# Branch B's mask sums on GpSimd: made one unit ahead, behind the scaling of the unit in front

## The chip, the cores and the metric

The kernel runs on one core of a Trainium2 chip. The metric is the device time of one execution in microseconds (us). The engines are named as the profile names them: PE is TensorE, DVE VectorE, ACT ScalarE, POOL GpSimd, SP SyncE. Each engine works through its own list of instructions in order, and an instruction starts when the semaphores that it waits for have come.

## What is computed

One encoder layer over two sequences, of 1024 and of 512 tokens. Its token mixer has two branches, and the change lies in branch B: attention in a two-dimensional neighbourhood, where each query sees a window of keys on a grid of 64 columns, with a learned bias by relative position. Per block of queries:

```python
s = jnp.einsum('bqhd,bkhd->bhqk', qi, kb, preferred_element_type=jnp.float32) * scale + bias[None]
s = jnp.where(mask[None, None], s, NEG_INF)
p = jax.nn.softmax(s, axis=-1)
return jnp.einsum('bhqk,bkhd->bqhd', p.astype(vb.dtype), vb)
```

Around it stand the norms, the projections, branch A (grouped-query attention over all tokens), sigmoid gates on both branches, the output projection, and an MLP with squared relu. All of it is float32; the kernel keeps that precision by splitting each operand into a high and a low part and adding three products.

## The kernel before

The kernel first runs the token mixer of the short sequence (first trunk, 512 tokens), then that of the long one (second trunk, 1024 tokens), then the MLP over all 1536 tokens. In each trunk branch B is a loop over **units**. A unit is one head with one strip of 16 grid columns and both halves of the rows (second trunk: 8 heads x 4 strips in the order 1, 2, 0, 3, that is 32 units) or one head with two strips (first trunk: strips 1 and 2, then 0 and 3, that is 16 units). Either way a unit has two score products, x = 0 and 1.

`s_unit(u)` makes, for x = 0 and 1 one after the other:

- the mask sum `bm` on GpSimd (line 993): the head's relative bias, gathered for 128 queries in the tile `rect`, plus the mask `msk`, which holds 0 or -1e30. Strip 2 uses the sums of strip 1, so there are 24 sums in the first trunk (128x256) and 48 in the second (128x384). There are four buffers for them;
- the score product on PE (line 1007, two matmuls, high and low part of the keys) into one half of the PSUM tile `s`, which both x share;
- on VectorE `tensor_tensor_reduce` (line 1009): scores plus mask sum, negated, with the row's extreme in `nm_`;
- on ScalarE the exponential with the row's sum (line 1013), on VectorE the reciprocal of the sum (line 1016), on GpSimd the scaling of the row (line 1017).

`t_unit`, one unit later, transposes the scaled rows on PE (lines 1032 and 1038) and splits them into high and low part on ScalarE and VectorE (lines 1041 and 1042). `v_unit`, two units later, multiplies them with the values (line 1064) and adds the parts up (VectorE line 1071, GpSimd line 1084). Between these steps PE is given matmuls of the gate and of the query, key and output projections (`fill`), and VectorE and ScalarE the splits of those weights (lines 198 and 192). `prep(h)` loads `rect` (line 908, two buffers) and the head's value strips (line 914) on SyncE's queue.

The order on the engines is not the order of the code. A scheduler moves instructions on each engine by its own estimate of when they can start, except those that `tc.keep_in_program_order` pins to their place behind what was issued before them on the engine. The mask sums were not pinned: the scheduler put them as far ahead as their four buffers allow, which on GpSimd often means between two scalings of an earlier unit.

Of the kernel before, what the change touches and what calls it, by code (L numbers as in the profile page):

```python
# [11 lines left out]
F32 = mybir.dt.float32  # L12
# [3 lines left out]
ALU = mybir.AluOpType  # L16
AX = mybir.AxisListType

P = 128
# [42 lines left out]
def encoder(ctx: ExitStack, tc: tile.TileContext, xs, outs, w):  # L62
    nc = tc.nc
# [32 lines left out]
    def big(name):  # L96
        return pbig.tile([P, 1024], F32, tag="big", name=name)
# [84 lines left out]
    def rstd(ss, n, width, name, pin=False):  # L182
        m = sml.tile([P, 8], F32, tag="ms", name=f"ms_{name}")
        op = nc.vector.tensor_scalar(m[:, :n], ss, 1.0 / width, EPS, op0=ALU.mult, op1=ALU.add)  # L184
        if pin:
            tc.keep_in_program_order(op)
        r = sml.tile([P, 8], F32, tag="rs", name=f"rs_{name}")
        nc.gpsimd.tensor_tensor(r[:, :n], m[:, :n], mhalf[:, :n], op=ALU.pow)  # L188
        return r
# [240 lines left out]
    def run(tr, nxt, first):  # L430
        N, x, T, NT, NB = tr.N, tr.x, tr.T, tr.NT, tr.NB
        xh, xl = tr.xh, tr.xl
        rows = T // GRID_W
        halves = rows // 8
# [70 lines left out]
        for g in range(2):  # L505
            with phase(f"phR{N}_{g}") as ph:
# [154 lines left out]
                for tt in range(NT):  # L661
                    tb, j = divmod(tt, 4)
                    nm = f"{N}_{g}_{tt}"
# [13 lines left out]
                    op = nc.sync.dma_start(rt, w["rope"][tt * P : (tt + 1) * P])  # L677
# [3 lines left out]
                    js = slice(j * P, (j + 1) * P)  # L681
# [28 lines left out]
                    r = rstd(ss[:, :5], 5, HD, f"A{nm}", fresh and tt < 2 if first else ahead_)  # L710
# [61 lines left out]
            with phase(f"phA{N}_{g}") as ph:  # L772
                units = [(h, qb) for h in range(4) for qb in range(NB)]
# [40 lines left out]
                for ui, u in enumerate(units):  # L814
                    h, qb = u
# [81 lines left out]
        kr_n = 12 if halves == 2 else 8  # L897
        nkc = kr_n // 4
        nkey = kr_n * 32
        nq = rows * 16  # L900
        with phase(f"phB{N}") as ph:
            msk = ph.tile([P, halves * 3, nkey], BF16, tag="msk", name=f"msk{N}", bufs=1)
            nc.gpsimd.dma_start(msk, w["mask2"] if halves == 2 else w["mask1"])
            rects, strips, bms, PT = {}, {}, {}, {}

            def prep(h):
                rc = ph.tile([P, 16, 48], F32, tag="rect", name=f"rect{N}_{h}", bufs=2)
                nc.sync.dma_start(rc, biases[:, :, h].rearrange("r c i j -> (r c) i j"))
                rects[h] = rc
                v = slot([P, 4, rows // 4, P], F32R, f"vs{N}_{h}")  # L910
                for j in range(4):
                    c0 = (0, 8, 24, 32)[j]
                    for a in range(4):
                        nc.sync.dma_start(
                            v[a * 32 : a * 32 + 32, j, :, :].bitcast(F32),
                            vd[:, h, :].rearrange("(k a c) d -> a c k d", a=4, c=GRID_W)[a, c0 : c0 + 32],
                        )
                strips[h] = v

            def load_qk(pr, hold=None):  # L920
                return (
                    load_cols(win, 768 + pr * P, P, f"bq{N}_{pr}", hold=hold),
                    load_cols(win, 1280 + pr * P, P, f"bk{N}_{pr}", hold=hold),
                )
# [49 lines left out]
            JN = 3 - halves  # L974
            W = halves * P

            def s_unit(u):
                h, js = u
                s = big(f"sb{N}_{h}_{js[0]}")
                p = ph.tile([P, 2, nkey], F32, tag="pb", name=f"pb{N}_{h}_{js[0]}", bufs=2)  # L980
                nm_, l, rl = (
                    sml.tile([P, 8], F32, tag=n_, name=f"{n_}b{N}_{h}_{js[0]}") for n_ in ("ms", "ss", "rs")
                )
                for x, (j, hf) in enumerate((j, hf) for j in js for hf in range(halves)):
                    nm = f"{N}_{h}_{j}_{hf}"
                    ct = (0, 1, 1, 2)[j]
                    c0 = (0, 8, 24, 32)[j]
                    jr = (16, 8, 8, 0)[j]
                    r0 = 0 if hf == 0 else 4
                    ir = 4 if hf == 0 else 0  # L990
                    if j != 2:
                        bm = ph.tile([P, nkey], F32, tag="bm", name=f"bm{nm}", bufs=4)
                        nc.gpsimd.tensor_tensor(
                            bm.rearrange("p (r c) -> p r c", c=32),
                            rects[h][:, ir : ir + kr_n, jr : jr + 32],
                            msk[:, hf * 3 + ct, :].rearrange("p (r c) -> p r c", c=32),
                            op=ALU.add,
                        )
                        bms[hf] = bm
                    bm = bms[hf]  # L1000
                    q0 = j * (T // 4) + hf * P
                    so = s[:, x * 512 : x * 512 + nkey]
                    for i in range(2):
                        kv = qk[h // 2][1][h % 2][:, i, :].rearrange("p (r c) -> p r c", c=GRID_W)[
                            :, r0 : r0 + kr_n, c0 : c0 + 32
                        ]
                        nc.tensor.matmul(so, qk[h // 2][0][:, h % 2, q0 : q0 + P], kv, start=(i == 0), stop=(i == 1))
                    sb = ph.tile([P, nkey], F32, tag="sb", name=f"sbs{nm}", bufs=2)
                    nc.vector.tensor_tensor_reduce(
                        out=sb, in0=so, in1=bm, op0=ALU.add, op1=ALU.min, scale=-1.0, scalar=3e38,  # L1010
                        accum_out=nm_[:, x : x + 1],
                    )
                    nc.scalar.activation(
                        p[:, x], sb, AF.Exp, bias=nm_[:, x : x + 1], scale=-1.0, accum_out=l[:, x : x + 1]
                    )
                    nc.vector.reciprocal(rl[:, x : x + 1], l[:, x : x + 1])
                    nc.gpsimd.tensor_scalar(p[:, x], p[:, x], rl[:, x : x + 1], 1.0, op0=ALU.mult, op1=ALU.mult)
                PT[u] = p
# [87 lines left out]
            units = [(h, js) for h in range(8) for js in groups]  # L1106
            n = len(units)
# [4 lines left out]
            for i in range(n + LS + LV):  # L1112
                if NB == 1:
                    f = 9 if i < 1 else 5 if i < n - 4 else 6 if i < n else 4 if i == n else 2
                else:
                    f = 0 if i == n - 10 else 5 + (i % 3 > 0) if i < n - 8 else 7
                if i < n:
                    s_unit(units[i])
                    if units[i][1][0] == 1 and units[i][0] + 1 < 8:
                        prep(units[i][0] + 1)  # L1120
                    if i % per == (6 if JN == 1 else 2) and i + 2 < n:
                        while held:
                            held.pop(0)()
                        qp = qkproj(i // per + 1, wqk, qk)
                        for _ in range(NC8):
                            next(qp)
                    if i % per == per - 1 and qp is not None:
                        for _ in qp:
                            pass
                        qp = None  # L1130
                fill.pull(f // 2)
                if 0 <= i - LS < n:
                    t_unit(units[i - LS])
                if held:
                    held.pop(0)()
                if i % per == 0 and i // per < 3:
                    wqk = load_qk(i // per + 1, held)
                if i == n - (6 if first else 9):
                    pa = proj_a(ph, held)
                    next(pa)  # L1140
                if i == n - (4 if JN == 2 else 8):
                    fill.drain()
                    fill.add(pa)
                if qp is not None and NB == 2:
                    for _ in range(NC8):
                        next(qp)
                fill.pull(f - f // 2)
                if 0 <= i - LS - LV < n:
                    v_unit(units[i - LS - LV])
# [4 lines left out]
        with phase(f"phG{N}") as ph:  # L1154
# [36 lines left out]
            for c in range(NC8):  # L1191
# [4 lines left out]
                for tb in range(NB):  # L1196
# [4 lines left out]
                    nm = f"{N}_{c}_{tb}"  # L1201
# [33 lines left out]
            for half in range(2):  # L1235
                wo = wos[half]
                hc = slice(half * 512, half * 512 + 512)
                for tt in range(NT):
                    tb, j = divmod(tt, 4)
                    nm = f"{N}_{half}_{tt}"  # L1240
# [34 lines left out]
                    for k, i in todo:  # L1275
                        js = slice(i * P, (i + 1) * P)
# [13 lines left out]
                    if ht is not None:  # L1290
                        op = nc.vector.tensor_tensor(ht[:, hc], o, xr, op=ALU.add)
# [12 lines left out]
                    if half == 1:  # L1304
# [5 lines left out]
                        if nxt is None:  # L1310
# [10 lines left out]
                            if 3 <= tt <= 5:  # L1321
                                j = tt - 3
# [557 lines left out]
    for i, tr in enumerate(trunks):  # L1880
        run(tr, trunks[i + 1] if i + 1 < len(trunks) else None, i == 0)
# [66 lines left out]
```

## Time and profile before

| | us |
|---|---|
| runs | 2135.02, 2132.51, 2131.47 (median 2132.51) |
| profiled execution | 2131.02 |
| its span, first to last instruction | 2129.2 |
| POOL busy in the span | 390.7 |
| branch B's loop, first trunk | about 165 to 300 us of the span |
| branch B's loop, second trunk | about 785 to 1050 us of the span |

In the rows of the profile a group reads: line, engine, operation, output tile <- input tiles (buffer numbers left out), shape, count, then busy time and the mean of one in ns, then the idle time of the engine just before and what ended it. In the timeline a row begins with the start in us and the duration in us; what stands in square brackets is the engine's idle time before it and what ended that. Tiles of branch B: `sbs` the scores in PSUM, `sbss` the negated sums, `msbs` their extremes, `bms` the mask sums, `pbs` the exponentials, `rsbs` the reciprocals, `ptbs` the transposes, `bhs` their parts, `obs` and `os_Bs` the outputs. A matmul of 512 columns starts some 0.23 us after the one before it when nothing waits, a 128x128 transpose behind another some 0.11 us.

### The profile page before, as it was taken

How to read it: one execution, taken by the hardware profiler on the slowest of the kernel's cores; microseconds unless marked ns; L12 is line 12 of the kernel's file. 1: busy time of each engine (PE TensorE's matmuls, PEld its weight loads, DVE VectorE, ACT ScalarE, POOL GpSimd, SP SyncE). 2: the span in 40 equal slices, each digit the busy share in tenths (PEclk: the TensorE clock that was granted, in tenths of full speed). 3: DMA queues.
4: the chain of work that ended last, by engine and by line, in shares of the span. 5: the costliest groups of instructions: out<-in, count | busy, mean ns of one | idle time of the engine just before them, and what ended most of it. 6: DMA issues, size and time to landing. Idle time of an engine off the chain costs nothing.

```text
span 2129.2 us, 31802 instructions
## 1 busy us (share of the span) xinstructions
PE 2111.4 (99%) x10967; PEld 1847.8 (87%) x10967; DVE 1471.0 (69%) x2810; ACT 1117.3 (52%) x2351; POOL 390.7 (18%) x508
## 2 busy tenths in 40 slices
PE   9999999999999999999999999999999999999998
PEld 8887788988898888888888999999999988888887
DVE  6674686777667754656782977778777777769563
ACT  5664564566537644655431566566555643434352
POOL 3332420433233323433300200003000000000000
PEclk9999999999999999999999999999999999999999
DMA  6445567521221132433472666578444799688561
GB/s 188 136 125 146 156 192 243 189 72 34 59 85 55 40 110 84 124 105 109 142 247 101 212 197 200 155 247 210 159 146 158 260 353 343 214 279 281 168 197 70
DMA packets 319595, 350.92 MB, mean 165 GB/s; under 512 B 31168, under 2 KB 255048, under 8 KB 319433
## 3 DMA queue, kind: packets, MB, share of 16 engines
q1 hardware_dynamic: 277495, 278.86, 41.7%
q10 hardware_dynamic: 36258, 52.98, 7.1%
q0 software_dynamic: 5680, 17.04, 2.9%
q8 instruction: 87, 1.43, 0.3%
q14 instruction: 75, 0.61, 0.1%
HBM read 264.85 MB, written 87.88 MB: 166 GB/s over the span
## 4 chain that ended last, share of the span: by engine, by line
PE 82%; DVE 2%; DMA 1%; issue 1%; ACT 1%; POOL 1%; SPq 0%; ACTq 0%; POOLq 0%; DVEq 0%
PE dn L205 7%; PE dn L203 7%; PE dn L204 7%; PE pTs L827 3%; PE gpss L203 3%; PE gpss L205 3%; PE gpss L204 3%; PE ud L205 2%; PE uc L205 2%; PE ud L204 2%; PE uc L204 2%; PE uc L203 2%; PE ud L203 2%; PE ua L205 2%; PE ua L204 2%; PE ua L203 2%
## 5 line engine op out<-in xcount | busy, mean ns | idle before, releaser
L205 PE MATMUL dn<-wd,al 128*128 128x512 f32 (+1 forms) x624 | 242.6, 389 | 0.0
L204 PE MATMUL dn<-wd,ah 128*128 128x512 f32 (+1 forms) x624 | 242.6, 389 | 0.0
L203 PE MATMUL dn<-wd,ah 128*128 128x512 f32 (+1 forms) x624 | 242.6, 389 | 0.0
L1361 ACT ACTIVATE ah<-ar 128x512 fp32r<-128x512 f32 x168 | 104.7, 628 | 205.8 <-PE dn L204 181.7
L1362 DVE TENSOR_TENSOR al<-ar,ah 128x512 fp32r<-128x512 f32 x168 | 115.4, 692 | 77.8 <-ACT ah L1361 69.4
L204 PEld LDWEIGHTS dn<-wd,ah 128*128 128x128 f32 x624 | 117.2, 188 | 24.3
L205 PEld LDWEIGHTS dn<-wd,al 128*128 128x128 f32 x624 | 117.2, 188 | 24.1
L203 PEld LDWEIGHTS dn<-wd,ah 128*128 128x128 f32 x624 | 117.2, 188 | 24.0
L793 POOL TENSOR_SCALAR ps<-ps,rls 128x1024 f32<-128x1024 f32 (+1 forms) x96 | 96.8, 1010 | 215.6 <-DVE rls L792 205.0
L833 DVE TENSOR_TENSOR ptls<-pTs,pths 128x512 fp32r<-128x512 f32 x160 | 107.7, 686 | 39.3 <-ACT pths L832 38.8
L832 ACT ACTIVATE pths<-pTs 128x512 fp32r<-128x512 f32 x160 | 94.2, 598 | 74.0 <-PE pTs L827 72.1
L787 DVE TENSOR_REDUCE nms<-ss 128x1 f32<-128x1024 f32 (+1 forms) x96 | 99.6, 1039 | 22.2 <-PE ss L785 21.9
L188 POOL TENSOR_TENSOR rs_f<-ms_f,mhalf 128x1 f32<-128x1 f32 x6 | 4.0, 667 | 590.7 <-DVE ms_f L184 590.7
L203 PE MATMUL gpss<-xs_0h,w_gs 128*128 128x512 f32 x256 | 104.9, 410 | 1.5 <-DVE ptls L833 1.3
L790 ACT ACTIVATE ps<-ss,nms 128x1024 f32<-128x1024 f32 (+1 forms) x96 | 93.2, 972 | 23.1 <-DVE nms L787 20.3
L827 PEld LDWEIGHTS pTs<-ident,ps 128*128 128x128 f32 x640 | 78.2, 140 | 28.0 <-POOL ps L793 4.2
L204 PE MATMUL gpss<-xs_0l,w_gs 128*128 128x512 f32 x256 | 101.1, 395 | 0.0
L205 PE MATMUL gpss<-xs_0h,w_gs 128*128 128x512 f32 x256 | 101.0, 395 | 0.0
L827 PE MATMUL pTs<-ident,ps 128*128 128x128 f32 x640 | 98.9, 274 | 1.2 <-DVE ptls L833 0.3
L1361 ACT ACTIVATE A<-S 128x512 fp32r<-128x512 f32 x128 | 76.1, 624 | 30.5 <-DVE S L1424 26.2
L1362 DVE TENSOR_TENSOR A<-S,A 128x512 fp32r<-128x512 f32 x128 | 84.5, 685 | 3.9 <-ACT A L1361 3.9
L1480 ACT ACTIVATE c<-c 128x384 f32<-128x384 f32 x97 | 50.7, 524 | 68.7 <-DVE c L1479 68.6
(352 smaller groups left out, 6403.6 us busy)
## 6 DMA issues: line engine op xcount, KB each, us to landing
ar<-ud SPq DMA_DIRECT2D x120, 512.0 KB
br<-in_w_mlp_down_dram SPq DMA_DIRECT2D x72, 512.0 KB
rawu<-in_w_mlp_up_dram SPq DMA_DIRECT2D x64, 512.0 KB
ud<-c ACTq DMA_DIRECT2D x128, 192.0 KB
raw_gs<-in_w_in_dram SPq DMA_DIRECT2D x32, 512.0 KB
zgs<-sgs ACTq DMA_DIRECT2D x48, 256.0 KB
ud<-cs SPq DMA_DIRECT2D x64, 192.0 KB
raw_os<-in_w_out_dram SPq DMA_DIRECT2D x16, 512.0 KB
```

The costliest lines, as they stand in the source:

```text
L203: nc.tensor.matmul(out, ah, bh, start=start, stop=False, **kw)
L204: nc.tensor.matmul(out, ah, bl, start=False, stop=False, **kw)
L205: nc.tensor.matmul(out, al, bh, start=False, stop=stop, **kw)
L787: nc.vector.tensor_reduce(nm_, s, axis=AX.X, op=ALU.max, negate=True)
L790: nc.scalar.activation(p, s, AF.Exp, bias=nm_, accum_out=l)
L793: nc.gpsimd.tensor_scalar(p, p, rl, 1.0, op0=ALU.mult, op1=ALU.mult)
L827: nc.tensor.transpose(pt[:, j * P : (j + 1) * P], PP[u, j][:, kc * P : (kc + 1) * P], ident)
L832: nc.scalar.activation(hi, pt, AF.Copy)
L833: nc.vector.tensor_tensor(lo, pt, hi.bitcast(F32), op=ALU.subtract)
L1361: nc.scalar.activation(hi, src, AF.Copy)
L1362: nc.vector.tensor_tensor(lo, src, hi.bitcast(F32), op=ALU.subtract)
L1480: nc.scalar.activation(t, t, AF.Relu)
```

## The change

The sums of a unit are moved out of `s_unit` into a function of their own, `masks(u)`. It is called for unit 0 ahead of the loop's first step and for unit i + 1 right after `s_unit` of unit i, and its sums are pinned, so that on GpSimd they stand behind the scalings of unit i. The dictionary of the sums is keyed by unit. The sums themselves, their shapes and their four buffers are the same.

```diff
+            def masks(u):
+                h, js = u
+                for j, hf in ((j, hf) for j in js for hf in range(halves)):
+                    if j == 2:
+                        bms[u, j, hf] = bms[(h, (1,)) if len(js) == 1 else u, 1, hf]
+                        continue
+                    ct = (0, 1, 1, 2)[j]
+                    jr = (16, 8, 8, 0)[j]
+                    ir = 4 if hf == 0 else 0
+                    bm = ph.tile([P, nkey], F32, tag="bm", name=f"bm{N}_{h}_{j}_{hf}", bufs=4)
+                    tc.keep_in_program_order(
+                        nc.gpsimd.tensor_tensor(
...
+                    bms[u, j, hf] = bm
...
-                    if j != 2:
-                        bm = ph.tile([P, nkey], F32, tag="bm", name=f"bm{nm}", bufs=4)
-                        nc.gpsimd.tensor_tensor(
...
-                        bms[hf] = bm
-                    bm = bms[hf]
+                    bm = bms[u, j, hf]
...
+                if i == 0:
+                    masks(units[0])
                 if i < n:
                     s_unit(units[i])
+                    if i + 1 < n:
+                        masks(units[i + 1])
```

What this does to the order on the engines is shown at three places. In the rows a tile's name ends in head, strip and (for a mask sum) half, and then a running number; line 993 is line 990 after the change, line 1007 is 1017, 1017 is 1027, 1032 is 1042 and 1084 is 1094.

On GpSimd, at the start of the first trunk's branch B, before:

```order
L993 TENSOR_TENSOR bms_0_1_0_2264<-rects_0_2151,msks_2149 128x256
L993 TENSOR_TENSOR bms_0_0_0_2351<-rects_0_2151,msks_2149 128x256
L993 TENSOR_TENSOR bms_0_3_0_2360<-rects_0_2151,msks_2149 128x256
L993 TENSOR_TENSOR bms_1_1_0_2403<-rects_1_2280,msks_2149 128x256
L1017 TENSOR_SCALAR pbs_0_1_2260<-pbs_0_1_2260,rsbs_0_1_2263 128x256
L993 TENSOR_TENSOR bms_1_0_0_2515<-rects_1_2280,msks_2149 128x256
L1017 TENSOR_SCALAR pbs_0_1_2260<-pbs_0_1_2260,rsbs_0_1_2263 128x256
```

and after:

```order
L990 TENSOR_TENSOR bms_0_1_0_2259<-rects_0_2151,msks_2149 128x256
L1027 TENSOR_SCALAR pbs_0_1_2262<-pbs_0_1_2262,rsbs_0_1_2265 128x256 x2
L990 TENSOR_TENSOR bms_0_0_0_2280<-rects_0_2151,msks_2149 128x256
L990 TENSOR_TENSOR bms_0_3_0_2282<-rects_0_2151,msks_2149 128x256
L1027 TENSOR_SCALAR pbs_0_0_2351<-pbs_0_0_2351,rsbs_0_0_2354 128x256 x2
L990 TENSOR_TENSOR bms_1_1_0_2369<-rects_1_2284,msks_2149 128x256
```

Before, the sums of strips 0 and 3 of head 0 and one of head 1 stood ahead of the first scaling; now they stand behind the scalings of the unit in front.

On GpSimd in the second trunk, from the output sum of head 0, strip 1, before:

```order
L1084 TENSOR_TENSOR os_Bs_0_1_9291<-os_Bs_0_1_9291 64x256
L1017 TENSOR_SCALAR pbs_0_3_9296<-pbs_0_3_9296,rsbs_0_3_9299 128x384
L993 TENSOR_TENSOR bms_1_0_1_9530<-rects_1_9116,msks_8915 128x384
L1017 TENSOR_SCALAR pbs_0_3_9296<-pbs_0_3_9296,rsbs_0_3_9299 128x384
L1084 TENSOR_TENSOR os_Bs_0_2_9356<-os_Bs_0_2_9356 64x256
L1017 TENSOR_SCALAR pbs_1_1_9361<-pbs_1_1_9361,rsbs_1_1_9364 128x384 x2
```

and after, from the scalings of the same unit:

```order
L1027 TENSOR_SCALAR pbs_0_3_9300<-pbs_0_3_9300,rsbs_0_3_9303 128x384 x2
L990 TENSOR_TENSOR bms_1_1_0_9318<-rects_1_9116,msks_8915 128x384
L990 TENSOR_TENSOR bms_1_1_1_9320<-rects_1_9116,msks_8915 128x384
L1094 TENSOR_TENSOR os_Bs_0_2_9360<-os_Bs_0_2_9360 64x256
L1027 TENSOR_SCALAR pbs_1_1_9365<-pbs_1_1_9365,rsbs_1_1_9368 128x384 x2
```

Before, a sum for two units later stood between the two scalings of unit 0_3; now the two sums of the next unit, 1_1, stand behind them.

On PE, in the first trunk, from the first score product of unit 0_0 (strips 0 and 3 of head 0) to its second, before:

```order
L1007 MATMUL sbs_0_0_2346<-kBs_0_0_2189,qBs_0_2188 128x256 x2
L203 MATMUL gpss_3328_1_0_2342<-xs_0h_158,w_gs_3328_1_2301 128x512
L204 MATMUL gpss_3328_1_0_2342<-xs_0l_160,w_gs_3328_1_2301 128x512
L205 MATMUL gpss_3328_1_0_2342<-xs_0h_158,w_gs_3328_1_2301 128x512
L203 MATMUL gpss_3328_1_0_2342<-xs_0h_158,w_gs_3328_1_2301 128x512
L204 MATMUL gpss_3328_1_0_2342<-xs_0l_160,w_gs_3328_1_2301 128x512
L1007 MATMUL sbs_0_0_2346<-kBs_0_0_2189,qBs_0_2188 128x256 x2
L205 MATMUL gpss_3328_1_0_2342<-xs_0h_158,w_gs_3328_1_2301 128x512
L1032 MATMUL ptbs_0_1_2376<-ident,pbs_0_1_2260 128x128 x4
```

and after:

```order
L1017 MATMUL sbs_0_0_2350<-kBs_0_0_2189,qBs_0_2188 128x256 x2
L203 MATMUL gpss_3328_1_0_2346<-xs_0h_158,w_gs_3328_1_2305 128x512
L204 MATMUL gpss_3328_1_0_2346<-xs_0l_160,w_gs_3328_1_2305 128x512
L205 MATMUL gpss_3328_1_0_2346<-xs_0h_158,w_gs_3328_1_2305 128x512
L203 MATMUL gpss_3328_1_0_2346<-xs_0h_158,w_gs_3328_1_2305 128x512
L204 MATMUL gpss_3328_1_0_2346<-xs_0l_160,w_gs_3328_1_2305 128x512
L205 MATMUL gpss_3328_1_0_2346<-xs_0h_158,w_gs_3328_1_2305 128x512
L1042 MATMUL ptbs_0_1_2378<-ident,pbs_0_1_2262 128x128 x2
L1017 MATMUL sbs_0_0_2350<-kBs_0_0_2189,qBs_0_2188 128x256 x2
L1042 MATMUL ptbs_0_1_2378<-ident,pbs_0_1_2262 128x128 x2
```

The second score product stands one matmul and two transposes further back. The same happens in the first trunk to units 2_0, 3_1, 4_0, 6_0 and 7_1 (in 4_0 by one matmul and three transposes, in 3_1 by eight matmuls, in 6_0 by nine matmuls and four transposes), and in the second trunk to unit 0_0 alone (by two matmuls). Everywhere else PE's order is the same apart from the numbers in names. VectorE's order moves at those same places only. On SyncE the loads of `rect` stand further back, behind the value strips or weight loads that they stood before.

More of the change, by code (lines that the diff above doesn't have):

```diff
@@ L903, in run @@
             nc.gpsimd.dma_start(msk, w["mask2"] if halves == 2 else w["mask1"])
-            rects, strips, bms, PT = {}, {}, {}, {}
+            rects, strips, PT = {}, {}, {}
             def prep(h):
@@ L975, in run @@
             W = halves * P
+            bms = {}
+            def masks(u):
[10 more added lines that the diff above has]
+                        nc.gpsimd.tensor_tensor(
+                            bm.rearrange("p (r c) -> p r c", c=32),
+                            rects[h][:, ir : ir + kr_n, jr : jr + 32],
+                            msk[:, hf * 3 + ct, :].rearrange("p (r c) -> p r c", c=32),
+                            op=ALU.add,
+                        )
+                    )
+                    bms[u, j, hf] = bm
             def s_unit(u):
@@ L985, in s_unit @@
                     nm = f"{N}_{h}_{j}_{hf}"
-                    ct = (0, 1, 1, 2)[j]
                     c0 = (0, 8, 24, 32)[j]
-                    jr = (16, 8, 8, 0)[j]
                     r0 = 0 if hf == 0 else 4
-                    ir = 4 if hf == 0 else 0
-                    if j != 2:
-                        bm = ph.tile([P, nkey], F32, tag="bm", name=f"bm{nm}", bufs=4)
[L993 to L998, printed above, removed]
-                        bms[hf] = bm
-                    bm = bms[hf]
+                    bm = bms[u, j, hf]
                     q0 = j * (T // 4) + hf * P
```

## The prediction

> **What bounds the kernel now.** I read the page first, then the waits of TensorE and GpSimd, then the timeline at places where one unit of branch B hands over to the next.
>
> ```profile
> span 2129.2 us, 31802 instructions
> PE 2111.4 (99%) x10967; PEld 1847.8 (87%) x10967; DVE 1471.0 (69%) x2810; ACT 1117.3 (52%) x2351; POOL 390.7 (18%) x508
> PE 82%; DVE 2%; DMA 1%; issue 1%; ACT 1%; POOL 1%; SPq 0%; ACTq 0%; POOLq 0%; DVEq 0%
> ```
>
> TensorE (PE) is busy all but 17.8 us of the span (2129.2 - 2111.4), and the chain that ended last is 82% PE. GpSimd (POOL) is busy 18%. So a mask sum can change the time only where PE comes to wait for it. Branch B runs twice: the 512-token trunk and the 1024-token trunk, in these two windows.
>
> ```profile
> 165.00:300.00 135.00, 132.67 (x654) 107.35 (x653) 86.70 (x233) 75.43 (x155) 47.01 (x69) 1.00 0.52 154
> 785.00:1050.00 265.00, 262.35 (x1281) 215.85 (x1281) 167.56 (x435) 145.18 (x308) 101.02 (x138) 1.00 0.37 113
> ```
>
> The first two numbers behind a window are its length and PE's busy time: PE idles 2.33 us in the first and 2.65 us in the second, at a granted clock of 1.00. Nearly all of that would have to vanish to win 0.2%. What PE waits for there:
>
> ```profile
> PE sbs L1007 <- DVE msbs L1009: 1.7, 5, 0.5
> PE ptbs L1038 <- POOL pbs L1017: 0.6, 1, 0.6
> ```
>
> The five waits of 1.7 us are the core of the case. A unit has two score products in one PSUM tile, and the second (QK2) starts only when VectorE has read the first together with its mask sum (DVE1). A late mask therefore becomes a PE wait. GpSimd itself, in the second window:
>
> ```profile
> L993 POOL TENSOR_TENSOR bms<-rects,msks 128x384 f32<-128x384 f32 x44 | 41.9, 953 | 71.7 <-DVE msbs L1009 71.7
> L1017 POOL TENSOR_SCALAR pbs<-pbs,rsbs 128x384 f32<-128x384 f32 x64 | 39.1, 612 | 37.2 <-DVE rsbs L1016 30.7 <-ACT pbs L1013 2.0 <-ACT bhs L1041 1.4
> ```
>
> The masks run so far ahead that GpSimd stands 71.7 us waiting for one of the four mask buffers (released by L1009), and the scalings stand behind those waits. No mask is late for VectorE anywhere.
>
> **The change, part by part.** The same 72 sums and 96 scalings remain; nothing is computed twice. What moves: the sums of unit u+1 stand directly behind the scalings of unit u. Their buffers are then long free, so the 71.7 us of waiting goes; in exchange a loop closes through five engines: QK2 of u, VectorE's second read, exponential, reciprocal, scaling, mask of u+1, DVE1 of u+1, QK2 of u+1. I check each hand-over by one formula: end of the second scaling, plus one mask, against the traced start of DVE1. QK2 follows DVE1 closely, so what is late goes to PE in full.
>
> Second trunk, the tightest hand-over (unit 0_3 to unit 1_1):
>
> ```profile
> 808.67 0.16 DVE L1016 RECIPROCAL rsbs<-ssbs 128x1 f32<-128x1 f32 x1 [0.69 <-ACT pbs L1013]
> 808.93 0.58 POOL L1017 TENSOR_SCALAR pbs<-pbs,rsbs 128x384 f32<-128x384 f32 x1
> 809.91 0.56 DVE L1009 CUSTOM_DVE_ANT_0 sbss<-sbs,bms 128x384 f32<-128x384 f32 x1 [1.08 <-PE sbs L1007]
> 810.40 0.08 DVE L1009 DVE_READ_ACCUMULATOR2_ANT msbs<- 128x1 f32 x1
> 810.54 0.61 PE L1007 MATMUL sbs<-kBs,qBs 128*128 128x384 f32 x2
> ```
>
> The scaling starts 0.10 behind its reciprocal and ends at 809.51; a mask of 0.92 (the row at 793.89 below) ends at 810.43, 0.52 behind DVE1's traced start, and QK2 stood only 0.06 behind DVE1's end (810.48). So PE waits 0.5 us. Order on PE and VectorE is unchanged here. The same formula, at the four others that come out late:
>
> ```profile
> 867.67 0.57 POOL L1017 TENSOR_SCALAR pbs<-pbs,rsbs 128x384 f32<-128x384 f32 x1
> 868.69 0.56 DVE L1009 CUSTOM_DVE_ANT_0 sbss<-sbs,bms 128x384 f32<-128x384 f32 x1 [0.69 <-PE sbs L1007]
> 873.73 0.59 POOL L1017 TENSOR_SCALAR pbs<-pbs,rsbs 128x384 f32<-128x384 f32 x1 [1.32 <-DVE rsbs L1016]
> 875.00 0.56 DVE L1009 CUSTOM_DVE_ANT_0 sbss<-sbs,bms 128x384 f32<-128x384 f32 x1 [0.44 <-issue]
> 880.00 0.59 POOL L1017 TENSOR_SCALAR pbs<-pbs,rsbs 128x384 f32<-128x384 f32 x1 [1.31 <-DVE rsbs L1016]
> 881.30 0.56 DVE L1009 CUSTOM_DVE_ANT_0 sbss<-sbs,bms 128x384 f32<-128x384 f32 x1 [0.48 <-issue]
> 944.85 0.59 POOL L1017 TENSOR_SCALAR pbs<-pbs,rsbs 128x384 f32<-128x384 f32 x1 [0.17 <-DVE rsbs L1016]
> 945.92 0.55 DVE L1009 CUSTOM_DVE_ANT_0 sbss<-sbs,bms 128x384 f32<-128x384 f32 x1
> ```
>
> 868.24 + 0.92 against 868.69 is 0.47 late; the next three, in the same way, 0.24, 0.21 and 0.44. At all others of this trunk the mask ends before DVE1 starts. Sum: 0.52 + 0.47 + 0.24 + 0.21 + 0.44 = **+1.9 us**.
>
> The start of the second trunk has a stall that goes:
>
> ```profile
> 793.89 0.92 POOL L993 TENSOR_TENSOR bms<-rects,msks 128x384 f32<-128x384 f32 x1 [0.54 <-DVE msbs L1009]
> 794.78 0.58 POOL L1017 TENSOR_SCALAR pbs<-pbs,rsbs 128x384 f32<-128x384 f32 x1
> 795.42 0.55 PE L1038 MATMUL ptbs<-ident,pbs 128*128 128x128 f32 x3 [0.65 <-POOL pbs L1017]
> 795.85 0.16 DVE L1016 RECIPROCAL rsbs<-ssbs 128x1 f32<-128x1 f32 x1 [0.29 <-ACT pbs L1013]
> 797.90 0.52 PE L1007 MATMUL sbs<-kBs,qBs 128*128 128x384 f32 x2
> ```
>
> A mask at 793.89 held the scaling, and with it the transposes, by 0.65; that goes. But next on PE is QK2 of unit 0_0, two matmuls later than before, at 797.90 - 0.65 + 2 x 0.23 = 797.7. Its mask now follows the scaling behind the reciprocal of 795.85: 796.1 + 0.58 + 0.92 = 797.6, DVE1 until 798.2, so PE waits about 0.55 there. Net **-0.1 us**.
>
> First trunk. The scheduler has moved QK2 back in six of the 16 units; the order shows the first. Unit 0_0:
>
> ```profile
> 187.46 0.67 DVE L198 TENSOR_TENSOR w_bqs<-raw_bqs,w_bqs 128x512 fp32r<-128x512 f32 x1
> 187.64 0.84 POOL L1017 TENSOR_SCALAR pbs<-pbs,rsbs 128x256 f32<-128x256 f32 x1 [0.72 <-DVE rsbs L1016]
> 188.05 0.41 DVE L1009 CUSTOM_DVE_ANT_0 sbss<-sbs,bms 128x256 f32<-128x256 f32 x1
> 188.55 1.05 POOL L993 TENSOR_TENSOR bms<-rects,msks 128x256 f32<-128x256 f32 x1
> 188.52 0.51 PE L1007 MATMUL sbs<-kBs,qBs 128*128 128x256 f32 x2 [0.19 <-DVE msbs L1009]
> ```
>
> The mask cannot start before 188.48. At 0.67 it ends at 189.15, DVE1 at 189.6, QK2 starts near 189.7; PE reaches it at 188.6 (one matmul and two transposes later than before). PE waits 1.1 instead of some 0.35 (188.52 less 188.17, where the matmul before was due to end its pitch): +0.75, and +1.15 if the mask takes 1.05. I take **+0.9**. Unit 4_0 (250 us) repeats it, 3_1 (224 us) gives some back, 6_0 (282 us) comes out even:
>
> ```profile
> 250.22 1.36 POOL L1017 TENSOR_SCALAR pbs<-pbs,rsbs 128x256 f32<-128x256 f32 x2
> 250.97 0.42 DVE L1009 CUSTOM_DVE_ANT_0 sbss<-sbs,bms 128x256 f32<-128x256 f32 x1
> 251.45 0.51 PE L1007 MATMUL sbs<-kBs,qBs 128*128 128x256 f32 x2 [0.25 <-DVE msbs L1009]
> 251.56 0.67 POOL L993 TENSOR_TENSOR bms<-rects,msks 128x256 f32<-128x256 f32 x1
> 224.43 0.50 PE L1007 MATMUL sbs<-kBs,qBs 128*128 128x256 f32 x2 [0.45 <-DVE msbs L1009]
> 282.55 0.51 PE L1007 MATMUL sbs<-kBs,qBs 128*128 128x256 f32 x2 [0.41 <-DVE msbs L1009]
> ```
>
> 251.58 + 0.67 = 252.25, 1.28 behind DVE1's 250.97; QK2 stands 0.56 later in the order (one matmul, three transposes), so PE waits some 1.2 instead of 0.4: **+0.8**. At 224.43 QK2 moves eight matmuls back (1.8 us), more than the mask's delay: the wait goes, **-0.5**. At 282.55 nine matmuls and four transposes (2.5 us) stand against a mask that by the formula is late by as much: **0**. The other two moved units (2_0, 7_1) I also cost at 0. The sum over both trunks: 0.9 + 0.8 - 0.5 + 1.9 - 0.1 = **+3.0 us**.
>
> The loads of the bias tile (L908) wait for the mask sum that last reads its buffer, and stand in SyncE's queue before the value strips (L914) and weight loads.
>
> ```profile
> SPq L908 <- POOL bms L993: 34.8, 7, 12.1
> ```
>
> These sums come up to a unit or two later, but the scheduler has put the loads behind others that were issued later anyway; by the formula above the worst case holds the strips back by 1.2 us, and none of PE's waits in the trace is for a strip. I cost it at 0; with that cover gone it would be 1.2.
>
> What the rows leave open is how long a mask takes where it lands.
>
> ```profile
> L993 POOL TENSOR_TENSOR bms<-rects,msks 128x256 f32<-128x256 f32 x24 | 18.0, 754 | 31.1 <-DVE msbs L1009 20.3 <-DMA rects<-biases 8.2 <-DVE rsbs L1016 2.5
> ```
>
> The mean is 0.754 in the first trunk (0.953 in the second); single masks take 0.67 undisturbed and 1.05 beside a VectorE split from two SBUF tiles (the L198 row stands next to the 1.05 above), so +0.4 for each of about fourteen tight hand-overs, at most +5.6; below, all the quoted waits on msbs (0.19, 0.45, 0.25, 0.41) and the 0.65 could vanish with no mask late, -2.0. I keep the middle, nearest the undisturbed rows, and both ends.
>
> The Trainium skill, page "SBUF — State Buffer", section "Who interferes with whom", says that a VectorE operation with two SBUF inputs and a GpSimd operation that reads SBUF exclude each other for a whole instruction. The 1.05 and the 0.84 beside L198 agree with it; by it, masks that meet a split come late by most of a split, which is rival B.
>
> **Rivals.**
> A, faster: the freed GpSimd lets scalings start so early that masks are still in time. Against it: the scaling at 808.93 already started right behind its reciprocal. It decides if the second scalings end 0.5 us (second trunk) or 1.2 us (first) sooner than traced. Price -2.0, in the extreme the 5.0 us of idle: 2130.5.
> B, slower: the mask, now behind the scaling that comes just after a reciprocal, meets VectorE's splits as a rule. It decides from a mean mask time above about 0.8 in the first and 1.1 in the second trunk at the tight hand-overs. Price 3.0 + 2 to 5.6, so about +6.5: 2139.0.
> C, no effect: each hand-over has cover that the formula doesn't see (DVE1 is late anyway for its own queue): 2132.5.
>
> **How the numbers follow.** Against the profiled execution (2131.02 us, its span 2129.2 and 1.8 around it) the sum gives 2134.0; the median of the runs shown, 2132.51, is 1.5 above that execution, so I predict **2135.5**. Chances: forecast (+1 to +4.5) 0.42, B 0.26, A 0.17, C 0.15. The range takes in -2.0 and +8.6 around the median, rounded outwards below: 2130 to 2141. A measurement of this kernel can tell about 0.2%, 4.3 us, from no change. Slower than that: most of B and a little of the forecast, 0.26; faster: the far end of A, 0.06; within: 0.68.
>
> **What would show it.** Right: VectorE waiting for POOL bms before L1009 (not there before), GpSimd's waits on msbs gone, PE's wait "sbs <- msbs" up from 1.7 to some 4 us in more places, the wait at 795.42 gone. Rival B: mean mask time above 754 and 953 ns. Wrong: PE busy and idle as before, or masks ending before VectorE asks.

## The result, and the profile after

The changed kernel takes 2140.05 us (median of 6 runs, 2139.62 to 2143.29), the kernel before 2132.82 (6 runs, 2131.47 to 2135.02). The ratio is 1.0036, 95% interval 1.0026 to 1.0046: about 7 us or 0.36% slower, which is above the 0.2% that a measurement can tell. The predicted 2135.5 was 4.6 us too low; the range up to 2141 held the time near its upper end; and "slower by over 0.2%" had been given 0.26.

The page of the changed kernel (profiled execution 2139.86 us), rows as in the prediction:

```profile
span 2138.1 us, 31794 instructions
PE 2115.4 (99%) x10967; PEld 1847.2 (86%) x10967; DVE 1471.3 (69%) x2810; ACT 1118.0 (52%) x2351; POOL 389.7 (18%) x508
PE 48%; DVE 1%; DMA 1%; issue 1%; ACT 0%; POOL 0%; POOLq 0%; ACTq 0%; DVEq 0%
```

The span grew by 8.9 us. PE's idle time grew by only 4.9 (2138.1 - 2115.4 = 22.7 against 17.8). Since the ends of matmuls are modelled, part of a wait can count as busy, so I go by the starts of instructions below. The shares of the chain add up to 51%: it was followed back over half of the span only, so it is not the row to compare. Work per engine is the same to within 0.3%. The waits of PE, and of VectorE for mask sums:

```profile
PE sbs L1017 <- DVE msbs L1019: 6.1, 13, 1.1
...
PE ptbs L1042 <- POOL pbs L1027: 1.1, 1, 1.1
...
PE ptbs L1048 <- POOL pbs L1027: 0.2, 1, 0.2
```

```profile
DVE sbss L1019 <- POOL bms L990: 17.6, 15, 2.0
```

The last row has no counterpart before: the profile now puts 15 waits of VectorE, 17.6 us in all, down to mask sums. For five of them, some 6.5 us, that is not so: the sums had ended 0.36 to 0.58 us before, and VectorE started 0.13 us behind the end of its score product. The longest is one of these; its sums were done at 946.24, and VectorE and PE read

```profile
946.61 0.56 DVE L1019 CUSTOM_DVE_ANT_0 sbss<-sbs,bms 128x384 f32<-128x384 f32 x1 [2.00 <-POOL bms L990]
```

```profile
945.96 0.52 PE L1017 MATMUL sbs<-kBs,qBs 128*128 128x384 f32 x2
```

So VectorE waits for a mask sum some ten times, about 11 us in all. PE's waits for VectorE's reads rose from 1.7 us (5 waits) to 6.1 (13). GpSimd's groups, grouped by shape in the windows of the two trunks:

```profile
L990 POOL TENSOR_TENSOR bms<-rects,msks 128x256 f32<-128x256 f32 x24 | 17.7, 753 | 6.8 <-DMA rects<-biases 6.8
```

```profile
L990 POOL TENSOR_TENSOR bms<-rects,msks 128x384 f32<-128x384 f32 x46 | 41.9, 932 | 0.0
```

The sums wait for no buffer any more (71.7 us before in the second trunk), and one takes as long as before: 753 and 932 ns against 754 and 953. To place the loss, take the first score product of the second trunk, in the timeline of before and of after:

```profile
787.87 0.45 PE L1007 MATMUL sbs<-kBs,qBs 128*128 128x384 f32 x1
```

```profile
793.63 0.45 PE L1017 MATMUL sbs<-kBs,qBs 128*128 128x384 f32 x1
```

5.8 us were lost by then. From the first to the last score product, the first trunk takes 112.9 us before and 118.3 after, the second 254.2 and 256.6; those two lengths, read from the timeline in the same way, serve for all experiments below. The other 1.1 us of the span's growth lie outside these stretches, in parts of 0.1 to 0.7; the same parts differ by as much, and by up to 1.5, between the runs below.

### The profile page after: what moved, and what is told of

It reads as the page before. It is cut to its first block, busy times and chain, and to the rows that moved or that the text cites. A ratio compares the mean times of both kernels' runs of the same rounds, so it can differ in the third digit from the quotient of the medians.

```text
span 2138.1 us, 31794 instructions
## 1 busy us (share of the span) xinstructions
PE 2115.4 (99%) x10967; PEld 1847.2 (86%) x10967; DVE 1471.3 (69%) x2810; ACT 1118.0 (52%) x2351; POOL 389.7 (18%) x508
## 4 chain that ended last, share of the span: by engine, by line
PE 48%; DVE 1%; DMA 1%; issue 1%; ACT 0%; POOL 0%; POOLq 0%; ACTq 0%; DVEq 0%
PE dn L205 7%; PE dn L203 7%; PE dn L204 7%; PE ud L203 2%; PE uc L203 2%; PE uc L205 2%; PE ud L205 2%; PE uc L204 2%; PE ud L204 2%; PE ua L205 2%; PE ua L203 2%; PE ua L204 2%; PE ops L205 1%; PE ops L204 1%; PE ops L203 1%; PE ub L205 1%
## 5 line engine op out<-in xcount | busy, mean ns | idle before, releaser
L204 PEld LDWEIGHTS dn<-wd,ah 128*128 128x128 f32 x624 | 117.1, 188 | 24.3
L205 PEld LDWEIGHTS dn<-wd,al 128*128 128x128 f32 x624 | 117.1, 188 | 24.2
L203 PEld LDWEIGHTS dn<-wd,ah 128*128 128x128 f32 x624 | 117.1, 188 | 24.1
```

The source lines that it names most:

```text
L203: nc.tensor.matmul(out, ah, bh, start=start, stop=False, **kw)
L204: nc.tensor.matmul(out, ah, bl, start=False, stop=False, **kw)
L205: nc.tensor.matmul(out, al, bh, start=False, stop=stop, **kw)
```

## The experiments

**Theory 1**: a sum that stands behind the second scaling of the unit in front ends after VectorE asks for it, and what it makes late goes round the loop again. **Rivals**: the order that the scheduler then gives to PE and VectorE costs the time, not the lateness; or the pin or the moved code does.

| kernel | median, us | ratio to before, 95% interval | first trunk, us | second trunk, us |
|---|---|---|---|---|
| before (beside the other kernels 2132.3 to 2132.6) | 2132.82 | | 112.9 | 254.2 |
| after | 2140.05 | 1.0036, 1.0026 to 1.0046 | 118.3 | 256.6 |
| e1_ahead | 2134.37 | 1.0008, 0.9999 to 1.0017 | 113.5 | 255.7 |
| e2_unpinned | 2131.86 | 0.9998, 0.9990 to 1.0007 | 113.0 | 254.2 |
| e3_first | 2137.78 | 1.0025, 1.0015 to 1.0035 | 118.2 | 254.4 |
| e4_second | 2134.40 | 1.0010, 1.0001 to 1.0018 | 112.9 | 256.6 |
| e7_double | 2154.78 | 1.0106, 1.0092 to 1.0120 | 125.5 | 263.9 |
| e5b_half | 2137.19 | 1.0023, 1.0014 to 1.0032 | 117.1 | 254.5 |
| e6_between | 2137.22 | 1.0024, 1.0015 to 1.0034 | 115.7 | 255.7 |
| e8_tail | 2134.70 | 1.0012, 1.0003 to 1.0021 | 115.3 | 254.3 |
| e9_ahead_part | 2131.84 | 0.9997, 0.9988 to 1.0007 | 112.5 | 253.8 |

All diffs are against the changed kernel.

### Without the pin

```diff
-                    tc.keep_in_program_order(
-                        nc.gpsimd.tensor_tensor(
...
-                        )
+                    op = nc.gpsimd.tensor_tensor(
...
                     )
```

> The changed kernel without the pin: the calls stay where the change put them in the code, but the scheduler places the sums itself, and on GpSimd they run ahead as before. Theory 1 (lateness): the time of before, 2131.5 to 2134, GpSimd's waits for its mask buffers back at about 90 us in both trunks, PE's wait sbs <- msbs near 1.7 us. Rival (the move of the code with its new keys and tile order costs it): stays at 2138 or above.

Measured 0.9998: the time of before, with both trunks at their old lengths and GpSimd waiting 91.2 us for its buffers again. The moved code and the new keys cost nothing; the loss is in where the pin puts the sums.

### One trunk at a time

```diff
+                    if NB == 1:
+                        tc.keep_in_program_order(op)
```

(`op` is the sum; NB is 1 in the first trunk, and e4 has `NB == 2`.)

> The pin in the first trunk alone; the second trunk's sums are placed by the scheduler. In the changed kernel's trace the second trunk's first score product starts 5.8 us later than before, and the stretch from there to its end is 2.2 us longer. Theory 1: the delays compound in the first trunk's bunched units, so this kernel keeps most of the loss: 2137 to 2139.5. By the terms of the prediction the first trunk would cost only 1.2: 2134. Rival (the clock, the DMA or what follows branch B carries the loss): the two halves don't add up to the whole.

> The pin in the second trunk alone. Theory 1, and the prediction's own term for it (+1.8): 2134 to 2136, some 2 us above before, with PE's new waits on msbs all behind 787 us. Rival (the loss is shared evenly by the number of sums, 24 to 48): about 5 us above before, 2137.5.

Measured 1.0025 and 1.0010, some 5.2 and 1.9 us over the runs of before beside them, which add up to the whole (7.1 against 7.2). The first trunk, with half as many sums, carries three quarters of the loss; the rivals of both runs fall.

### One unit sooner still

```diff
-                    s_unit(units[i])
                     if i + 1 < n:
                         masks(units[i + 1])
+                    s_unit(units[i])
```

> The sums of unit i + 1 are called, still pinned, ahead of s_unit(i): on GpSimd they stand ahead of the scalings of unit i, one unit sooner than in the changed kernel. Theory 1 (the loss is lateness: a sum that stands behind the second scaling of the unit in front ends after VectorE asks for it): with a unit's length of lead no sum is late, VectorE's waits for POOL bms before L1019 (17.6 us) go, PE's wait sbs <- msbs falls from 6.1 to below 2 us, and the time is that of before or a little under it, 2130.5 to 2133.5. Theory 2 (the pin itself, or the order that PE and VectorE got with it, costs the 7 us whatever the sums' place): 2137 to 2141.

Measured 1.0008, most of the loss gone under the same pin, so theory 2 falls. PE and VectorE have the order of before here as to score products, and PE's row reads

```profile
PE sbs L1017 <- DVE msbs L1019: 1.2, 3, 0.5
```

But 2134.37 is 0.9 above the range of theory 1. Most of what remains is the second trunk's 1.5 us. Matched instruction by instruction with before, PE's largest single loss there, 0.6 us, comes at one place, the first of these rows GpSimd's, the second VectorE's; the rest is in pieces of 0.1 to 0.2 us:

```profile
1038.13 1.79 POOL L990 TENSOR_TENSOR bms<-rects,msks 128x384 f32<-128x384 f32 x2
```

```profile
1038.65 1.55 DVE L1107 TENSOR_TENSOR oXs<-os_Bs,oXs 64x256 fp32r<-64x256 f32 x1
```

In the timeline of before the same subtraction (L1097 there) starts at 1036.82 and takes 0.56, with a scaling beside it but no sum. Beside two sums it takes 1.55, and behind it the splits, the reciprocal and the transposed scores' low part come late, which PE's output product then waits for. The groups of this subtraction over the whole run, before and here:

```profile
L1097 DVE TENSOR_TENSOR oXs<-os_Bs,oXs 64x256 fp32r<-64x256 f32 x12 | 6.8, 566 | 4.4 <-ACT oXs L1096 4.2
```

```profile
L1107 DVE TENSOR_TENSOR oXs<-os_Bs,oXs 64x256 fp32r<-64x256 f32 x12 | 8.4, 703 | 4.1 <-ACT oXs L1106 3.9
```

Two of the twelve in before take 1.23 already, beside one sum each; here three take 1.55. The mean is 436 ns in the changed kernel: there the sums stand where VectorE waits for them, and so beside no subtraction of this line.

### Each sum twice

```diff
-                    tc.keep_in_program_order(
-                        nc.gpsimd.tensor_tensor(
...
+                    for _ in range(2):
+                        tc.keep_in_program_order(
+                            nc.gpsimd.tensor_tensor(
...
```

> Each mask sum of the changed kernel is issued twice in a row (the second writes the same values), so a sum costs GpSimd some 1.35 us in the first trunk and 1.85 in the second, and the order on PE is that of the changed kernel but for a handful of projection matmuls and transposes. Theory 1 (lateness, and what is late goes round the loop again): the seven late places of the first trunk come later by 0.7 to 1.3 each, +5 to +12, and in the second trunk hand-overs that had up to 0.9 us of slack turn late too, +5 to +25; 2150 to 2175 in all, with VectorE's waits on POOL bms far above 17.6 us. Rival (the order that the scheduler gave to PE and VectorE costs the 7 us, not the lateness): the order is held, so 2139 to 2141.

Measured 1.0106, some 22 us: the loss is three times as large, with PE's order in branch B held but for four places. The rival that blames the order alone falls; what share of the 7 us the new order has is not shown by this run. At unit 0_0 GpSimd's two sums, each made twice, and PE's wait behind them read

```profile
188.73 2.78 POOL L991 TENSOR_TENSOR bms<-rects,msks 128x256 f32<-128x256 f32 x4
```

```profile
190.66 0.52 PE L1018 MATMUL sbs<-kBs,qBs 128*128 128x256 f32 x2 [1.60 <-DVE msbs L1020]
```

against a wait of 0.83 in the changed kernel (row below): one more sum of some 0.7 us, 0.77 more wait. PE's waits in all:

```profile
PE sbs L1018 <- DVE msbs L1020: 16.0, 16, 2.5
```

VectorE's waits that the profile puts down to sums doubled only (34.3 us, 32 times), less than the "far above" that I had expected. But here just two of them (3.5 us) end with a score product instead: those that a sum ended went from about 11 us to about 31.

### Half of each sum

```diff
-                    bm = ph.tile([P, nkey], F32, tag="bm", name=f"bm{N}_{h}_{j}_{hf}", bufs=4)
+                    bm = ph.tile([P, nkey // 2], F32, tag="bm", name=f"bm{N}_{h}_{j}_{hf}", bufs=4)
...
-                            rects[h][:, ir : ir + kr_n, jr : jr + 32],
-                            msk[:, hf * 3 + ct, :].rearrange("p (r c) -> p r c", c=32),
+                            rects[h][:, ir : ir + kr_n // 2, jr : jr + 32],
+                            msk[:, hf * 3 + ct, : nkey // 2].rearrange("p (r c) -> p r c", c=32),
...
-                        out=sb, in0=so, in1=bm, op0=ALU.add, op1=ALU.min, scale=-1.0, scalar=3e38,
+                        out=sb.rearrange("p (t k) -> p t k", t=2), in0=so.rearrange("p (t k) -> p t k", t=2), in1=bm.rearrange("p (t k) -> p t k", t=1).broadcast_to([P, 2, nkey // 2]), op0=ALU.add, op1=ALU.min, scale=-1.0, scalar=3e38,
```

> Left out: half of each mask sum. The sum covers the first half of the keys only and VectorE reads it for both halves, so a sum gets shorter. From the two shapes in the trace of the changed kernel (256 columns some 0.67 us, 384 some 0.92, undisturbed) an estimate is 0.42 for 128 and 0.55 for 192 columns, 0.25 and 0.37 less. The scheduler puts the second score product of units 0_0, 2_0, 3_1 and 7_1 back to its place of before; 4_0 and 6_0 stay moved. Theory 1: each late place gets earlier by one or two times 0.25 in the first trunk (5.3 to 5.8 us of loss become 2 to 4) and by 0.37 in the second (2 us become 0.3): 2134.5 to 2137, with PE's waits on msbs at 0_0 and 3_1 shorter but still there. Rival (order): the loss goes at 0_0 and 3_1 and stays at 4_0, some 2 us in all, 2134, and no longer depends on the sums.

```profile
L990 POOL TENSOR_TENSOR bms<-rects,msks 128x192 f32<-128x192 f32 x48 | 25.9, 559 | 7.1 <-DMA msks<-in_mask_dram 7.1
...
L990 POOL TENSOR_TENSOR bms<-rects,msks 128x128 f32<-128x128 f32 x24 | 12.0, 513 | 7.0 <-DMA rects<-biases 7.0
```

Measured 1.0023, 0.2 us above theory 1's range. The sums got shorter by 0.24 and 0.37 in the mean, as estimated. The second trunk's loss went from 2.4 to 0.3, as expected; the first's only from 5.3 to 4.1, just outside the expected 2 to 4. The scheduler had put the second score product of 2_0 back to its old place, and there PE now waits instead:

```profile
221.57 0.39 PE L1017 MATMUL sbs<-kBs,qBs 128*128 128x256 f32 x1 [0.48 <-DVE msbs L1019]
```

So at this unit moving the score product is not what costs: where it isn't moved, PE waits at it. And in the first trunk halving the sum takes away 1.2 of 5.3 us: the sum's own length is the smaller part of what is late.

### Between the two scalings

```diff
+                    if x == 0 and ahead is not None:
+                        masks(ahead)
```

(in `s_unit`, behind the scaling; `ahead` is the next unit, and the call behind `s_unit` is dropped.)

> The sums of unit i + 1 are pinned between the two scalings of unit i. Theory 1: they no longer wait for the second reciprocal, so VectorE's waits on POOL bms fall to below 5 us and PE's on msbs to 2 to 3 us; in exchange the second scaling stands behind one or two sums (0.67 to 1.85 us), and PE's transposes (L1044 and L1050 here) come to wait for POOL pbs: 2133.5 to 2137. Rival (order; PE's score products stand as before here but for unit 6_0): 2132 to 2133.

```profile
DVE sbss L1019 <- POOL bms L990: 2.3, 3, 1.0
```

Measured 1.0024, 0.2 us above the range of theory 1 and far from the rival's 2132 to 2133. VectorE's waits fell to 2.3 us and PE's on msbs to 2.5 in 4 waits, and the transposes wait 1.1 once, as expected. The first trunk still loses 2.7 us, although PE's score products stand as before but for unit 6_0, and 1.7 of it comes ahead of that unit: moved score products are not needed for a loss. What I had not expected is the second trunk's 1.5 us; the largest single piece, 0.6 us, comes behind these rows of GpSimd and VectorE:

```profile
1040.71 2.15 POOL L990 TENSOR_TENSOR bms<-rects,msks 128x384 f32<-128x384 f32 x2
```

```profile
1041.08 2.06 DVE L198 TENSOR_TENSOR w_pas<-raw_pas,w_pas 128x256 fp32r<-128x256 f32 x2
```

Before, the same two splits take 0.76 (at 1037.33), with no sum beside them. It is e1's cost at the same place, on another instruction.

### The last two heads of the first trunk alone

```diff
+                    if NB == 1 and h >= 6:
+                        tc.keep_in_program_order(op)
```

> The pin for heads 6 and 7 of the first trunk alone (units 6_1 to 7_0); every other sum is placed by the scheduler. In the changed kernel PE lost some 2.0 us from 276 us of the span to the end of the first trunk, where the prediction had put 0: the transposes of 6_1 waited 1.1, and the second score product of 7_0 waited 1.0. Theory 1a (the loop closes within two or three bunched units): the same waits appear, 2134 to 2135. Theory 1b (the lateness was carried over from the units of heads 0 to 5): the waits are halved or gone, below 2133.3.

Measured 1.0012, with the first trunk 2.4 us longer: theory 1a, the loop closes within two or three units. The waits of the changed kernel are there (that of the transposes shorter, 0.69):

```profile
285.12 0.44 PE L1042 MATMUL ptbs<-ident,pbs 128*128 128x128 f32 x2 [0.69 <-POOL pbs L1027]
...
286.55 0.51 PE L1017 MATMUL sbs<-kBs,qBs 128*128 128x256 f32 x2 [0.53 <-DVE msbs L1019]
```

```profile
296.01 0.51 PE L1017 MATMUL sbs<-kBs,qBs 128*128 128x256 f32 x2 [0.88 <-DVE msbs L1019]
```

### Ahead only where it gained

```diff
+                    if h < (6 if NB == 1 else 2):
+                        tc.keep_in_program_order(op)
...
-                    s_unit(units[i])
                     if i + 1 < n:
                         masks(units[i + 1])
+                    s_unit(units[i])
```

> The order of e1_ahead where its trace gained on before, and nowhere else: the sums of unit i + 1 ahead of s_unit(i), pinned for heads 0 to 5 of the first trunk and heads 0 and 1 of the second; the rest is placed by the scheduler. PE and VectorE keep the order of before. Matched instruction by instruction, e1_ahead gained 0.4 at 188 us, 0.5 at 224, 0.4 at 796 and 0.2 at 824 (all of them waits that a sum had caused by standing between two scalings or beside a split), and gave back 1.6 from 276 to 300 us and 2.0 from 1004 to 1050. Theory: the gains stay, the losses go: 1.0 to 1.5 us below before, 2131, a ratio of 0.9993 to 0.9997, which five rounds may not tell from none; the trace would show it in PE's waits. Rival (the gains are paid back later by what the sums then stand beside): the time of before or up to 2 us above it.

```profile
PE sbs L1017 <- DVE msbs L1019: 0.9, 3, 0.4
```

Measured 0.9997 (0.9988 to 1.0007): not told from before. In the trace both trunks are 0.4 us shorter, as the theory had it, and PE's waits on msbs halved from 1.7; the profiled span is not shorter (2130.7), since it differs by more outside the trunks. There is nothing worth having here: of PE's 17.8 us of idle time before, 5.0 lie in the windows of this loop.

## Why the prediction was too low

**What held.** GpSimd's waits for buffers went, VectorE's waits for sums came (some ten), PE's waits on msbs rose (to 6.1; I had said some 4), and the wait of the transposes at the start of the second trunk shrank from 0.65 to the 0.2 above. Unit 0_0, costed at +0.9, is the model case. After the change, GpSimd, VectorE and PE:

```profile
187.15 1.37 POOL L1027 TENSOR_SCALAR pbs<-pbs,rsbs 128x256 f32<-128x256 f32 x1 [1.30 <-DVE rsbs L1026]
188.49 1.29 POOL L990 TENSOR_TENSOR bms<-rects,msks 128x256 f32<-128x256 f32 x2
```

```profile
189.19 0.43 DVE L1019 CUSTOM_DVE_ANT_0 sbss<-sbs,bms 128x256 f32<-128x256 f32 x1 [0.94 <-POOL bms L990]
```

```profile
189.68 0.51 PE L1017 MATMUL sbs<-kBs,qBs 128*128 128x256 f32 x2 [0.83 <-DVE msbs L1019]
```

The prediction had the sum until 189.15, the score product near 189.7 and PE there at 188.6; it came at 189.68. PE's excess there (the time beyond the usual distance from the instruction before) is 1.08 against 0.36 before, so +0.7. Unit 4_0 came out in the same way (+0.8 predicted; its score product waits 0.65 longer than before and two of its transposes are held by 0.18).

**The second trunk was right in sum, not in its items.** Predicted +1.8; e4 alone gives +1.9, and the traces' lengths +2.4. The hand-over at 811 us cost 0.49 (0.52 predicted) and the start nothing (-0.1). The three at 868, 875 and 881 (0.92 together) cost some 0.2, and that at 946 only 0.18 of 0.44; in their place 0.5 to 0.6 came at 1014.6, where I had seen none, and the rest in pieces of 0.1 to 0.3, most of them behind 930 us. That the sum came out is luck.

**The step that failed** is the formula for the first trunk, "end of the second scaling, plus one mask, against the traced start of DVE1", with the end of the scaling taken as traced. It gave +1.2 there; the trunk lost 5.3, e3 alone 5.2. Where the units of a trunk stand close together, that end is itself an outcome of the change. Units 2_0 and 3_1 show it. Before (a score product of PE and VectorE's second read of 2_0, and its second scaling):

```profile
219.12 0.37 PE L1007 MATMUL sbs<-kBs,qBs 128*128 128x256 f32 x1
```

```profile
220.87 0.40 DVE L1009 CUSTOM_DVE_ANT_0 sbss<-sbs,bms 128x256 f32<-128x256 f32 x1
```

```profile
224.06 0.48 POOL L1017 TENSOR_SCALAR pbs<-pbs,rsbs 128x256 f32<-128x256 f32 x1 [0.48 <-DVE rsbs L1016]
```

After, on GpSimd, on VectorE and on PE:

```profile
220.16 1.77 POOL L990 TENSOR_TENSOR bms<-rects,msks 128x256 f32<-128x256 f32 x2
221.89 1.19 POOL L1094 TENSOR_TENSOR os_Bs<-os_Bs 64x256 f32<-64x256 f32 x1
...
226.17 0.48 POOL L1027 TENSOR_SCALAR pbs<-pbs,rsbs 128x256 f32<-128x256 f32 x1 [0.91 <-DMA vss<-vds]
226.61 0.67 POOL L990 TENSOR_TENSOR bms<-rects,msks 128x256 f32<-128x256 f32 x1
```

```profile
224.57 0.42 DVE L1019 CUSTOM_DVE_ANT_0 sbss<-sbs,bms 128x256 f32<-128x256 f32 x1
...
227.32 0.42 DVE L1019 CUSTOM_DVE_ANT_0 sbss<-sbs,bms 128x256 f32<-128x256 f32 x1
```

```profile
221.84 0.48 PE L1017 MATMUL sbs<-kBs,qBs 128*128 128x256 f32 x2
...
227.81 0.51 PE L1017 MATMUL sbs<-kBs,qBs 128*128 128x256 f32 x2 [1.13 <-DVE msbs L1019]
```

All times after are 0.9 us late by then. The scheduler moved 2_0's second score product back behind its late sum (221.84 against 219.12), which I had costed at 0 as PE doesn't wait there. But VectorE's second read of 2_0 moves back too, and further (224.57 against 220.87), then the scaling (226.17, 0.10 behind its reciprocal and not behind the load that the row names, against 224.06: 1.2 more than the delay so far), and then the sum of 3_1. The product is done at 222.32; but the read stands on VectorE behind the reciprocal for the unit's first score product, and that needs ScalarE's exponential for it:

```profile
223.11 0.63 ACTq L1096 DMA_DIRECT2D obds<-os_Bs  x1
223.78 0.51 ACT L1023 ACTIVATE pbs<-sbss,msbs 128x256 f32<-128x256 f32 x1 [2.06 <-DVE bhs L1052]
```

The exponential starts 0.04 behind ScalarE's issue of the store of the output, and that starts 0.03 behind the end of GpSimd's output sum (line 1094), which now stands behind the two mask sums. Before, the issue at 222.51 followed the output sum in the same way, but the exponential for the first product stood ahead of it, at 219.64. So the sums also delay ScalarE, by way of the output sum, which the formula had no term for; how much of the loss goes this way was not tried. So 3_1, with its score product eight matmuls further back, still waited 1.13; I had booked -0.5 for it and PE's excess rose by +0.7 (1.29 against 0.61). Moving a score product back hides the wait for its own sum and hands the delay to the next unit. In e8 the same happens to heads 6 and 7 alone.

At 6_0, costed at 0, a second thing was missed, in GpSimd's order: before, the scaling of 6_1 went ahead of the output sum; after, behind it. GpSimd before, GpSimd after, and PE after:

```profile
283.39 0.48 POOL L1017 TENSOR_SCALAR pbs<-pbs,rsbs 128x256 f32<-128x256 f32 x1
283.89 0.72 POOL L1084 TENSOR_TENSOR os_Bs<-os_Bs 64x256 f32<-64x256 f32 x1
```

```profile
286.99 0.87 POOL L1094 TENSOR_TENSOR os_Bs<-os_Bs 64x256 f32<-64x256 f32 x1 [0.92 <-POOL pbs L1027]
287.84 0.47 POOL L1027 TENSOR_SCALAR pbs<-pbs,rsbs 128x256 f32<-128x256 f32 x1
288.29 1.46 POOL L990 TENSOR_TENSOR bms<-rects,msks 128x256 f32<-128x256 f32 x2
```

```profile
288.37 0.44 PE L1042 MATMUL ptbs<-ident,pbs 128*128 128x128 f32 x2 [1.11 <-POOL pbs L1027]
```

The transposes of 6_1 wait 1.11 for that scaling, and the second score product of 7_0, two units on, 0.88 for what is late behind it. Together with 1_1 and 5_1 (PE's excess rose by 0.24 and 0.58, both costed at 0) and 0.3 at 279.6 us, where transposes wait for a VectorE split, this is where the first trunk's missing 4 us went.

**The rivals.** A (faster) and C (no effect) fell with the waits above. B had the right size, 2139.0, by the wrong mechanism: its sign was to be a longer mean sum, and 753 and 932 ns are not longer than before. That the range held the time is luck: its upper part was there for B. The collision that B rests on is real. One tight hand-over of the changed kernel shows it: the two sums at 220.16 take 1.77, beside a split, where those at 188.49 take 1.29. In the kernels that make the sums early it shows on the other engine too: in e1 and e6 VectorE's subtractions take 1.55 and 2.06 us instead of 0.56 and 0.76. The Trainium skill, page "SBUF — State Buffer", section "Who interferes with whom", says that a VectorE instruction with two SBUF inputs contends with a GpSimd instruction that reads SBUF; these rows agree. That the collision makes up all of e1's remaining 1.8 us was not tried by itself.

The loads of the bias tile, costed at 0, stayed without effect: none of PE's waits after the change is for a value strip.

## What to carry to other kernels

When a change puts a producer just in time behind a consumer's predecessor, the traced times of before are no longer inputs: close the loop (late read, late scaling, late next sum) and walk it over two or three units in the new order before summing, above all where the units are bunched. A wait that a scheduler hides by moving an instruction back is not free; look for who reads that instruction's result. An engine that runs far ahead and then waits for buffers lost nothing by it here (92 us of waits), and that lead was what kept PE fed. Pinning an instruction also moves what stands behind it on its engine: look who waits for that, down to the engine that issues a store of it.

## What the runs showed of the hardware

Two VectorE splits that take 0.76 us together alone took 2.06 beside two GpSimd sums of 2.15 (undisturbed some 1.8): VectorE lost 1.3 us, GpSimd 0.3. There a sum had started first (1040.71 against 1041.08). Beside the sums at 220.16 the split had started first:

```profile
220.07 0.69 DVE L198 TENSOR_TENSOR w_bqs<-raw_bqs,w_bqs 128x512 fp32r<-128x512 f32 x1 [0.62 <-ACT w_bqs L192]
```

It took 0.69, against 0.67 at 187.46 before, and the sums lost 0.5. In these rows the one that started second lost more.

ScalarE's issue of a store held the exponential behind it until GpSimd's output sum was done: 223.08, 223.11 and 223.78 in the rows above.

A sum's time falls by less than its size: half the columns took 513 ns instead of 753 (128x128), and 559 instead of 932 (128x192).
